# Sums of w_down's blocks made beside the q, k, v projection; a ring of their own for the sums of left blocks; squares of residual rows written to a row

## The chip, the core and the metric

The kernel runs on one core of a Trainium2 chip. The core has a matrix engine (TensorE, in the profile PE for matmuls and PEld for its weight loads), a vector engine (VectorE, DVE), a scalar engine (ScalarE, ACT), GpSimd (POOL) and SyncE (SP), which in this kernel issues every DMA. Each engine works through its own queue in order; semaphores hold an instruction until what it needs is there. The metric is the time of one execution on the device in microseconds, the median of several runs.

## The reference

One decoder layer over 2048 tokens of width 1024, all in float32:

```python
h = rmsnorm(x, g_mix);  z = h @ w_in                  # 1024 x 3072: conv columns and q, k, v
y_c = zb * causal_dwconv3(zc * zx, conv_w, conv_b)
y_a = dilated_attention(rmsnorm(q), rmsnorm(k), v)    # 8 heads, three dilated windows
x = x + concat(rmsnorm(y_c), rmsnorm(y_a)) @ w_out
h = rmsnorm(x, g_ffn)
gate = causal_dwconv3(h @ w_gate, ffn_conv_w, ffn_conv_b)
x = x + (silu(gate) * (h @ w_up)) @ w_down            # d_ff = 2816
x = x + sigmoid(rmsnorm(x, g_ple) @ w_ple_gate) * (p @ w_ple_proj)
```

## The kernel before

**Products.** Each float32 matrix is split in two parts, a high one (`hi`, made by a copy on ScalarE) and a low one (`lo`, the difference, made by VectorE or GpSimd); `split` (lines 90 to 92) does this, and `mm3` (94 to 99) multiplies with three matmuls: high by high, high by low, low by high. Matmuls are 128 x 128 by 128 x 512. The large products of the last part (`gate_up`, `down`, the gate of `ple`) use a scheme with seven instead of eight block products, for which sums and differences of blocks are made beforehand: the left operand's (`left`, 703), the right operand's (`right`, 728, seven tiles that are called the quad), and for `down` those of `silu(gate) * up` and of `w_down`.

**Stages.** `qkv` (first 334 us) goes over four chunks of 512 tokens (c) with four heads of work of 128 tokens each (j): `head` normalises x, transposes it, splits it and adds the two parts on GpSimd (line 174) to store h for the conv columns; `project` multiplies with w_q, w_k, w_v. `mix` then interleaves the conv group and the attention (to about 998 us). `rest` has the stages of line 655: `project` (the output projection, line 879; here and in the rest the name is that of the function in `rest`), `gate_up` for each half of the tokens (11 pairs f of 256 columns of d_ff, each with seven products for gate and seven for up), `down` for each half (seven products m of 11 f each), and `ple`. `prepare` and `for_later` are generators: `step()` takes one piece of them between products, as background work.

**w_down's sums.** `down` needs four sums of w_down's blocks (written to DRAM tiles `td`). They are made in `for_later`, the background of `gate_up 0`: eight pieces first normalise and transpose the other half's x into `bd`, then eleven pieces each load two blocks of w_down (256 rows), make four differences on GpSimd and store two tiles. All of these tiles come from the ring `operand("g")` (pool `rg`, four buffers of 4 KB a partition).

**Rings.** A tag's tiles go round in a fixed number of buffers. `row("t")` (pool `rx`, ten rows of 2 KB) serves in `gate_up` the four results t of each f and the three sums s1, s2, s4 of `combined` (a fourth is made in place), all of which go to DRAM (`gd`, lines 1015 and 1018); in `down` it serves the loads of gd (line 1041), which `split` turns into `operand("g")`; in `project` and `ple` rows of x and others. `row("u")` (pool `rs`, four rows) serves short-lived sums. `add_squares` (788) squares a row of the residual on ScalarE and adds it up; its elementwise result is not used and goes to `junk`, in `project` the PSUM bank of the product.

**Order.** The order of each engine's queue is not written by hand: the framework lays it out when the kernel is built, by the order of the code and by when it expects inputs and buffers to be there (`TileContext(nc, schedule_with_timeline_sim=True)`).

## Time and profile before

| | us |
|---|---|
| runs of the kernel before | 2870.42, 2872.03, 2878.88; median 2872.03 |
| profiled execution | 2883.12 |
| its span (first to last instruction) | 2881.3 |
| TensorE busy in the span | 2660.3 |
| q, k, v projection (0 to 334) | 334, TensorE 305.95 |
| mix (334 to 998) | 664, TensorE 607.33 |
| project (998 to 1251) | 253, TensorE 206.51 |
| gate_up 0 (1251 to 1724) | 473, TensorE 447.91 |
| down 0 (1724 to 1961) | 237, TensorE 216.38 |
| gate_up 1 (1961 to 2398.5) | 437.5, TensorE 432.18 |
| down 1 (2398.5 to 2645) | 246.5, TensorE 222.25 |
| ple (2645 to the end) | 236, TensorE 221.78 |

The table's stages are cut where TensorE changes from one group of tiles to the next. A busy matrix engine is not one at its peak: its clock has two levels, 2.4 and 1.2 GHz, and the share that was granted stands in the views by stretch as PEclk (1.00 is the upper level throughout). A row of a timeline gives start, duration, engine, line, operation, the tile written and the tiles read, how many like it were merged, and in brackets how long the engine was idle before it and what ended that.

### The profile page before, as it was taken

To read this page: it belongs to the slowest core of one execution; us is meant where nothing else is said; L and a number is where in the kernel's file an instruction comes from. 1 tells how busy PE (TensorE), PEld (TensorE's weight loads), DVE (VectorE), ACT (ScalarE), POOL (GpSimd) and SP (SyncE) were. 2 spreads that over 40 slices of the span, in tenths; PEclk is the share of its full clock that TensorE was granted. 3 is DMA by queue.
4 is the path that set the end of the run, shared out by engine and by line. 5 is a ranking of instruction groups with operands and counts; after the bars stand their busy time and mean duration, and the time that the engine had idled before them with its cause. 6 is when DMAs were issued, how large, how long until landed. Compare 5 with 4: busy or idle time off the path is not lost. (4 is left out here: it accounts for less than half of the span.)

```text
span 2881.3 us, 38272 instructions
## 1 busy us (share of the span) xinstructions
PE 2660.3 (92%) x12320; PEld 2194.4 (76%) x12320; DVE 2017.7 (70%) x3597; ACT 1291.1 (45%) x2699; POOL 1516.8 (53%) x1050
## 2 busy tenths in 40 slices
PE   6999989999999869799989998999999997998998
PEld 5777778888888757587767876877888886886777
DVE  7777656767676555978788777567888887657543
ACT  3332267776767234444333334453343334444332
POOL 4111311524344632446898667575666668667553
PEclk9999989999999989899999998999999998999999
DMA  6443666665765778544664237662232336674342
GB/s 182 147 139 117 183 152 145 184 167 156 188 160 160 192 258 275 162 166 146 233 217 154 91 127 235 218 228 92 99 106 99 103 109 211 228 240 160 96 127 77
DMA packets 374474, 470.11 MB, mean 163 GB/s; under 512 B 51072, under 2 KB 214528, under 8 KB 374272
## 3 DMA queue, kind: packets, MB, share of 16 engines
q1 hardware_dynamic: 374272, 467.66, 52.7%
q8 instruction: 97, 1.59, 0.2%
q14 instruction: 105, 0.86, 0.1%
HBM read 339.53 MB, written 127.99 MB: 162 GB/s over the span
## 5 line engine op out<-in xcount | busy, mean ns | idle before, releaser
L95 PE MATMUL ps<-t,w 128*128 128x512 f32 x4368 | 1040.9, 398 | 37.1 <-DVE u L766 19.1
L95 PEld LDWEIGHTS ps<-t,w 128*128 128x128 f32 x4368 | 824.7, 190 | 241.3 <-DVE u L766 22.2
L95 PE MATMUL ps<-w,g 128*128 128x512 f32 x2424 | 581.5, 401 | 77.3 <-ACT g L91 27.9
L92 POOL TENSOR_TENSOR w<-raw,w 128x512 fp32r<-128x512 f32 x318 | 469.7, 1483 | 322.5 <-ACT w L91 286.5
L95 PEld LDWEIGHTS ps<-w,g 128*128 128x128 f32 x2424 | 465.2, 194 | 187.5 <-ACT g L91 29.0
L92 POOL TENSOR_TENSOR w<-s,w 128x512 fp32r<-128x512 f32 x208 | 304.6, 1468 | 191.6 <-ACT w L91 182.8
L290 POOL TENSOR_TENSOR clo<-craw,chi 128x512 fp32r<-128x512 f32 x96 | 125.8, 1318 | 394.4 <-ACT chi L289 146.1
L91 ACT CAST w<-raw 128x512 fp32r<-128x512 f32 x318 | 196.0, 617 | 242.9 <-PE ps L95 157.6
L92 DVE TENSOR_TENSOR g<-t,g 128x512 fp32r<-128x512 f32 x154 | 207.8, 1360 | 126.4 <-ACT g L91 123.0
L95 PE MATMUL zps<-hq,chi 128*128 128x512 f32 x768 | 256.9, 412 | 7.4 <-DVE yc L329 5.0
L91 ACT CAST w<-s 128x512 fp32r<-128x512 f32 x208 | 128.0, 618 | 248.3 <-PE ps L95 179.7
L440 ACT ACTIVATE pt<-so,md 128x256 f32<-128x256 f32 (+1 forms) x384 | 175.0, 457 | 84.3 <-DVE md L437 82.3
L437 DVE CUSTOM_DVE_ANT_0 so<-s,neg 128x256 f32<-128x256 f32 (+1 forms) x384 | 130.5, 362 | 71.7 <-PE s L434 60.2
L95 PEld LDWEIGHTS zps<-hq,chi 128*128 128x128 f32 x768 | 142.3, 196 | 32.8 <-DVE yc L329 6.2
L95 PE MATMUL zps<-hq,clo 128*128 128x512 f32 x384 | 154.4, 403 | 0.0
L433 PE MATMUL s<-kk,qs 128*128 128x256 f32 (+1 forms) x384 | 134.4, 356 | 21.3 <-DMA kk<-kd 20.2
L434 PE MATMUL s<-kk,qs 128*128 128x256 f32 (+1 forms) x384 | 138.7, 365 | 15.2 <-DMA kk<-kd 9.6
L174 POOL TENSOR_TENSOR raw<-hT 128x1024 f32<-128x1024 f32 x16 | 39.0, 2440 | 202.2 <-DVE rs_h L78 187.4
L473 DVE TENSOR_TENSOR nb<-po,nb 64x512 f32<-64x512 f32 x96 | 92.2, 960 | 64.2 <-ACT nb L472 63.1
L1018 POOL TENSOR_TENSOR t<-t 128x512 f32<-128x512 f32 x88 | 126.5, 1449 | 5.9 <-DVE t L1010 3.2
L433 PEld LDWEIGHTS s<-kk,qs 128*128 128x128 f32 x384 | 106.9, 279 | 28.9 <-issue 14.5
L455 DVE TENSOR_TENSOR plo<-ptp,phi 128x512 fp32r<-128x512 f32 (+1 forms) x160 | 103.7, 654 | 32.0 <-ACT phi L454 31.1
(200 smaller groups left out, 4773.7 us busy)
## 6 DMA issues: line engine op xcount, KB each, us to landing
gd<-t SPq DMA_DIRECT2D x154, 256.0 KB, 2.0
t<-gd SPq DMA_DIRECT2D x154, 256.0 KB, 3.3
craw<-in_w_in_dram SPq DMA_DIRECT2D x96, 256.0 KB, 3.8
raw<-in_w_gate_dram SPq DMA_DIRECT2D x44, 512.0 KB, 3.9
raw<-in_w_up_dram SPq DMA_DIRECT2D x44, 512.0 KB, 3.6
raw<-td SPq DMA_DIRECT2D x40, 512.0 KB, 3.9
v<-vd SPq DMA_DIRECT2D x264, 64.0 KB, 2.5
kk<-kd SPq DMA_DIRECT2D x64, 256.0 KB, 8.0
```

The lines of the kernel that those rows point to most:

```text
L91: self.nc.scalar.copy(hi, src)
L92: lo_engine.tensor_tensor(lo, src, hi.bitcast(F32), ALU.subtract)
L95: mm = lambda *a, **k: self.nc.tensor.matmul(*a, **k, **kw)
L174: nc.gpsimd.tensor_tensor(t, hT[:, :, 0].bitcast(F32), hT[:, :, 1].bitcast(F32), ALU.add)
L290: nc.gpsimd.tensor_tensor(lo, raw, hi.bitcast(F32), ALU.subtract)
L433: mm(s[:, lo:], qb[l], cols[0], start=True, stop=False)
L434: mm(s[:, lo:], qb[l], cols[1], start=False, stop=True)
L437: nc.vector.tensor_tensor_reduce(out=so[:, lo:], in0=s[:, lo:], in1=neg[:, br, lo:], scale=-slope, scalar=3.0e38, op0=ALU.add, op1=ALU.min ...
L440: nc.scalar.activation(pt[:, l, lo:], so[:, lo:], AF.Exp, bias=md[:, 0, col:col + 1], scale=-1.0, accum_out=md[:, 1, col:col + 1])
L455: nc.vector.tensor_tensor(lo[:, i:i + n], tp[:, :n], hi[:, i:i + n].bitcast(F32), ALU.subtract)
L473: nc.vector.tensor_tensor(dst, like(po[other], br), dst, ALU.add)
L1018: nc.gpsimd.tensor_tensor(t, x, y, op)
```

## The change

Four edits. The eleven pieces of w_down's sums leave `for_later` and become `sums_of_w_down` in `qkv`, with two buffers of their own (tags `wd0`, `wd1`, one buffer each, 8 KB a partition together); one is called behind each of the first eleven heads of chunks 1 to 3. The sums s1, s2, s4 of `gate_up` get a pool of their own, `rk`, with three rows. To make room, ring `rg` goes from four buffers to three and ring `rx` from ten rows to nine. And the squares in `project` write to `row("u")` instead of the PSUM bank; the accumulator `sums` is renamed `squares`.

```diff
+            def sums_of_w_down(f):
+                b = [work.tile([P, 2, 512], F32, name="wd", tag=f"wd{i}", bufs=1) for i in range(2)]
+                for i, t in enumerate(b):
+                    n = (2 * f + i) * P
+                    nc.sync.dma_start(t.rearrange("p s n -> p (s n)"), a["w_down"][n:n + P])
+                minus = lambda t, x, y: nc.gpsimd.tensor_tensor(t, x, y, ALU.subtract)
+                (b11, b12), (b21, b22) = [[t[:, s] for s in range(2)] for t in b]
+                minus(b11, b12, b11)
+                minus(b12, b22, b12)
+                minus(b22, b22, b11)
+                minus(b21, b21, b22)
+                for d, t in zip(self.td, b):
+                    nc.sync.dma_start(d[f], t)
+
+            pairs = iter(range(NF // 2))
...
                     normed(project(hTs[j], 0), qn[j])
                     if c == 0 and j == 1:
                         load_w(1)
+                    for f in itertools.islice(pairs, int(c > 0)):
+                        sums_of_w_down(f)
...
-            late = pool("rg", bufs=4)
-            rows = pool("rx", bufs=10)
+            late = pool("rg", bufs=3)
+            rows = pool("rx", bufs=9)
+            sums = pool("rk", bufs=3)
...
-                                        add_squares(0, c, j, half, x, pss[j])
+                                        add_squares(0, c, j, half, x, row("u"))
...
-                minus = lambda t, x, y: nc.gpsimd.tensor_tensor(t, x, y, ALU.subtract)
-                for f in range(NF // 2):
-                    b1, b2 = wide(), wide()
-                    for i, b in enumerate((b1, b2)):
-                        n = (2 * f + i) * P
-                        nc.sync.dma_start(b.rearrange("p s n -> p (s n)"), a["w_down"][n:n + P])
-                    minus(b1[:, 0], b1[:, 1], b1[:, 0])
-                    minus(b1[:, 1], b2[:, 1], b1[:, 1])
-                    minus(b2[:, 1], b2[:, 1], b1[:, 0])
-                    minus(b2[:, 0], b2[:, 0], b2[:, 1])
-                    for t, b in zip(self.td, (b1, b2)):
-                        nc.sync.dma_start(t[f], b)
-                    yield
...
-                    s1, s2, s4 = (row("t") for _ in range(3))
+                    s1, s2, s4 = (sums.tile([P, 512], F32, name="c", tag="c") for _ in range(3))
```

## Rows read from the trace of the kernel before

**Rows 1.** The page: busy time of the engines (share of the span).

```profile
PE 2660.3 (92%) x12320; PEld 2194.4 (76%) x12320; DVE 2017.7 (70%) x3597; ACT 1291.1 (45%) x2699; POOL 1516.8 (53%) x1050
```

**Rows 2.** Busy time by stretch (instructions): gate_up 0's f = 2 to 6, one of gate_up 1.

```profile
core 0: us, PE busy (x) PEld busy (x) DVE busy (x) ACT busy (x) POOL busy (x), PEclk, DMA share, GB/s
1335.00:1377.50 42.50, 40.99 (x185) 33.05 (x184) 33.15 (x44) 16.91 (x29) 28.01 (x19) 1.00 0.45 155
1377.50:1428.60 51.10, 45.10 (x185) 35.94 (x184) 38.25 (x43) 17.13 (x29) 43.14 (x30) 0.90 0.66 235
1428.60:1478.40 49.80, 41.85 (x170) 33.34 (x169) 42.09 (x43) 14.72 (x24) 47.48 (x34) 0.90 0.65 213
1478.40:1523.90 45.50, 41.12 (x170) 32.51 (x169) 38.29 (x43) 15.27 (x25) 43.35 (x29) 0.96 0.68 229
1523.90:1566.60 42.70, 40.15 (x169) 31.00 (x168) 37.98 (x43) 15.24 (x26) 36.02 (x25) 1.00 0.44 155
2162.50:2201.80 39.30, 39.17 (x170) 31.52 (x169) 33.10 (x43) 15.08 (x25) 26.40 (x18) 1.00 0.30 100
1355.00:1550.00 195.00, 176.23 (x731) 140.10 (x730) 159.61 (x176) 66.51 (x112) 174.55 (x119) 0.94 0.61 211
```

**Rows 3.** Groups of POOL's instructions, 1355 to 1550 us: busy us, mean ns.

```profile
L965 POOL TENSOR_TENSOR g<-g 128x512 f32<-128x512 f32 x44 | 65.9, 1502 | 9.1 <-DMA g<-in_w_down_dram 8.8
```

**Rows 4.** Timeline of TensorE at the steps from gate_up to down.

```profile
1718.45 5.69 PE L95 MATMUL ps<-t,w 128*128 128x512 f32 x24 [0.87 <-DVE u L766]
1739.69 10.62 PE L95 MATMUL ps<-w,g 128*128 128x512 f32 x37 [15.55 <-ACT g L91]
...
2411.01 24.98 PE L95 MATMUL ps<-w,g 128*128 128x512 f32 x98 [12.36 <-ACT g L91]
```

**Rows 5.** Timeline of SP's DMA issues at the first of these steps.

```profile
1731.27 1.99 SPq L1015 DMA_DIRECT2D gd<-t  x2
1733.31 0.92 SPq L1041 DMA_DIRECT2D t<-gd  x2
```

**Rows 6.** Timeline of VectorE: the last result of up is taken from PSUM.

```profile
1726.28 0.68 DVE L1009 TENSOR_TENSOR u<-ps,u 128x512 f32<-128x512 f32 x1
...
2400.67 0.68 DVE L1009 TENSOR_TENSOR u<-ps,u 128x512 f32<-128x512 f32 x1
```

**Rows 7.** Busy time by stretch: the first step, and two of the projection (columns as above).

```profile
1727.00:1783.00 56.00, 40.60 (x161) 32.62 (x162) 42.94 (x34) 27.09 (x51) 42.76 (x28) 0.82 0.69 230
20.00:80.00 60.00, 48.05 (x196) 38.05 (x197) 55.34 (x139) 20.59 (x30) 29.04 (x12) 0.89 0.49 149
100.00:330.00 230.00, 226.02 (x1061) 182.43 (x1060) 170.06 (x510) 69.65 (x124) 41.89 (x22) 1.00 0.45 134
```

**Rows 8.** Timeline of POOL and VectorE in the projection.

```profile
117.76 2.44 POOL L174 TENSOR_TENSOR raw<-hT 128x1024 f32<-128x1024 f32 x1 [5.97 <-DVE rs_h L78]
...
117.95 2.34 DVE L80 TENSOR_SCALAR rs_y<-rs_i 128x8 int32<-128x8 int32 x2
```

**Rows 9.** Line 80 from 90 to 330 us: ns min/median/max.

```profile
L80 DVE TENSOR_SCALAR rs_y<-rs_i x34: 140/172/2300, 109.5 to 314.7; 128x8 int32<-128x8 int32 x24, 128x1 int32<-128x1 int32 x10
```

**Rows 10.** Timeline of SP's DMA issues at the start.

```profile
7.87 0.56 SPq L147 DMA_DIRECT2D gk<-in_k_norm_g_dram  x1
...
27.65 0.90 SPq L161 DMA_DIRECT2D raw<-in_w_in_dram  x2
```

**Rows 11.** Line 970, the 22 loads of w_down for the sums: time to landing.

```profile
DMA to landing us min/median/max: 3.3/4.8/5.4
```

**Rows 12.** What SP waited for, 1355 to 1560 us: in total, times, longest.

```profile
SPq L976 <- POOL g L965: 27.9, 16, 4.3
```

**Rows 13.** Timeline of ScalarE, VectorE and TensorE in the steady part of down 0.

```profile
1804.55 0.62 ACT L91 CAST g<-t 128x512 fp32r<-128x512 f32 x1
...
1805.26 1.31 DVE L92 TENSOR_TENSOR g<-t,g 128x512 fp32r<-128x512 f32 x1
...
1802.63 7.64 PE L95 MATMUL ps<-w,g 128*128 128x512 f32 x33
```

**Rows 14.** What TensorE waited for, whole span: in total, times, longest.

```profile
PE ps L95 <- DVE g L92: 9.8, 6, 2.7
```

More of the change, by code (lines that the diff above doesn't have):

```diff
@@ L784, in products @@
                 done(0, 1, z, u2)
-            sums = [cp.tile([P, 2, 4 * NQ], F32, name=f"sums{i}") for i in range(2)]
+            squares = [cp.tile([P, 2, 4 * NQ], F32, name=f"squares{i}") for i in range(2)]
             def add_squares(i, c, j, half, x, junk):
                 n = 4 * c + j
-                nc.scalar.activation(junk, x, AF.Square, accum_out=sums[i][:, half, n:n + 1])
+                nc.scalar.activation(junk, x, AF.Square, accum_out=squares[i][:, half, n:n + 1])
             def roots(i, first, n):
                 ss = tiny.tile([P, 8], F32, name="ssx", tag="ssx")[:, :n]
-                part = sums[i][:, :, first:first + n]
+                part = squares[i][:, :, first:first + n]
                 nc.vector.tensor_tensor(ss, part[:, 0], part[:, 1], ALU.add)
@@ L954, in for_later @@
                 r = roots(0, 8, 8)
-                wide = lambda: operand("g").bitcast(F32)
                 for j in range(4):
                     for i in range(2):
-                        x = wide().rearrange("p s n -> p (s n)")
+                        x = operand("g").bitcast(F32).rearrange("p s n -> p (s n)")
                         nc.sync.dma_start(x, self.xd[1][2 + i][j])
```

## The prediction

> **What bounds the kernel now.** I read the page first: TensorE is busy 92% of the span and no other engine over 70% [rows 1]. The change neither adds nor removes a matmul, so it can only move the time in which TensorE stands still or runs at its lower clock. Next I cut the span at the stages and looked for those with idle TensorE, and found two places that the change touches.
>
> The first lies in gate_up 0. An undisturbed f of gate_up 1 takes 39.3 us; in gate_up 0 four neighbouring f take 51.1, 49.8, 45.5 and 42.7 us [rows 2]. In the first three POOL is busy 84 to 95%, against 67% in the undisturbed f. POOL's groups of instructions there show what fills it: 44 subtractions for w_down's sums, 65.9 us [rows 3] of 174.6 busy in 195 us [rows 2]. POOL also makes the low part of each operand that TensorE waits for.
>
> The second is the step from gate_up to down, twice. TensorE stands 15.55 and 12.36 us, both times for ACT's split of g, and starts again slowly, with a lower granted clock [rows 7] (37 matmuls in 10.62 us against 24 in 5.69) [rows 4]. SP shows why: the first loads of g (t<-gd) are issued only behind the stores of the sums of the last f (gd<-t), and these wait for POOL [rows 5]. The "t" ring has ten rows; the last f holds seven, so three were free much earlier. That the loads came so late I take as a sign that rows of a tag are handed out in the order of the code: g comes after s1, s2, s4 of the last f.
>
> **The change, part by part.** The sum is made against the profiled execution, 2883.1 us (its span of 2881.3 and 1.8 around it), 0.4% over the median 2872.0 of the runs; the difference found is carried over to the median as a share.
>
> *A. The sums leave gate_up 0.* With 44 subtractions, 22 loads and 22 stores gone, nothing of for_later is left in f = 4 to 6, and f = 3 keeps only its 16 transposes, as the f before it, which took 42.5 us [rows 2]. Gain: (51.1 - 42.5) + (49.8 - 39.3) + (45.5 - 39.3) + (42.7 - 39.3) = 8.6 + 10.5 + 6.2 + 3.4 = 28.7 us. I take 29, ends 25 and 30. Nothing is late next: the same f of gate_up 1 runs at 39.17 busy of 39.30.
>
> *B. s1, s2, s4 get a ring of three; "t" has nine.* Four of the nine are the last f's, five are free, and in the order of the code g now follows the last f's gates. SP can issue five loads of g, and ACT and VectorE can split the three that the ring "g" takes, while TensorE is still at the last products. TensorE then waits only for its PSUM banks: the last result is taken out by 1727.0 and 2401.4 [rows 6], against starts at 1739.7 and 2411.0 [rows 4]. That is 12.7 + 9.6 = 22.3 us. With no long stall the clock stays up: 37 matmuls at 0.287 instead of 0.232 us and 98 at 0.255, 2.0 + 2.3 = 4.3 us. Together 26.6 at most. Against it: the background work (blocks for the next quad) still falls on these 56 us, in which VectorE was 42.9 and POOL 42.8 us busy [rows 7], and TensorE would now draw from them all through. I take 18, two thirds; ends 8 and 27.
>
> *C. The sums in the q, k, v projection (qkv).* Eleven pairs, one behind each head of c = 1 to 3 in the code. Each issues two loads and two stores of 512 KB on SP and four subtractions on POOL. POOL is not short: 41.9 of 230 us [rows 7]. VectorE is: 170 of 230 us there, and 55.3 of 60 us from 20 to 80 us [rows 7]. And POOL holds VectorE up: while the 2.44 us addition of L174 ran, two small instructions of L80 took 2.34 us, where the median of one is 0.17 and the longest 2.30 [rows 8, 9]. So an instruction of POOL costs VectorE between nothing and its whole length: 44 x 1.50 us [rows 3] = 66 us at most. I take half, 33.
> The Trainium skill, "SBUF — State Buffer", section "Who interferes with whom", has a rule against this change: GpSimd and some VectorE instructions (two SBUF inputs, or a two-port mode) lock a port pair for a whole instruction, and the other engine blocks fully. L80's rows agree in that the hold ends with POOL's instruction [rows 8]. By that rule alone the 66 us would stand whole, which is the third rival below.
> Where does it fall? Not where the code puts it. The loads of gk stand behind those of w1 and w2 in the code, and were issued at 7.9 us, ahead of w1's at 27.7 [rows 10]: work that waits for nothing is drawn forward. The sums wait for nothing but their two buffers. A pair takes a load (4.8 us to land [rows 11]), four subtractions (6.0 [rows 3]) and a store of the same size, some 15 us, so eleven reach from about 10 to 175 us. Four of them fall before 80 us: 16 x 0.75 = 12 us of VectorE's time against 4.7 idle, 7 on the path. Seven fall after: 28 x 0.75 = 21 us against an idle share of 26% of 95 us = 25, whose order does not fit exactly; a third, 7 us, on the path. The start also shares its DMA with 1 MB per pair, and on SP stand, behind each td store that waits for POOL, the next x loads, hd stores and spills; in gate_up 0 SP waited 27.9 us for those stores, 16 times [rows 12]. Another 3 us. Cost 17 us; ends 0 (all in idle time) and 58 (66 less a quarter of the 30 us idle).
>
> *D. Ring "g" of three, not four.* In down an operand takes 2.0 us from ACT's start to VectorE's end, and TensorE uses one for 12 x 0.232 = 2.8 us [rows 13]; its lead falls from about 6 (three more operands made, less 2.0) to 3.5 us. In steady stretches that is enough. With four, TensorE waited for VectorE's g six times, 9.8 us [rows 14]; each such place may grow by 2.8, 17 us at most, 0 at least. I take 8, the ple stage included, where a pair needs all three.
>
> *Answers at nothing.* Nine rows in project and in ple (a group takes four, so that two still fit), squares written to a "u" row instead of the PSUM bank (the bank comes free by one ACT instruction sooner; if "u" is short the square waits, not TensorE). The 8 KB more in the projection move the addresses of what follows; no row prices that, I leave 5 us either way in the range.
>
> Sum: -29 - 18 + 17 + 8 = -22 us, 2861 for a profiled execution, 0.76% less; of 2872.0 that leaves **2850**.
>
> **The rivals.** *All of it is won.* The sums fit into VectorE's gaps, the transitions close wholly: -29 - 27 + 3 = -53, 2819. For: from 100 us on TensorE had 226 of 230 us with VectorE a quarter idle [rows 7]. Against: 20 to 80 us.
> *The loads of g stay late.* If rows are not handed out in code order, or SP still has the stores in front, B does not do what it is meant to: -29 + 17 + 8 = -4, 2868, no change. For: SP issues in order, and 2 loads stood behind the first two stores. Against: the free rows.
> *The projection becomes bound by VectorE (slower).* Place: from 10 to 175 us. Each subtraction holds VectorE for its full length, and its instructions for the next head stand in a chain, so that only a quarter of the idle 30 us can be used: 66 - 8 = 58. With A, B and D as above -39 + 58 = +19, 2891. It decides from 48 us of cost on, 1.1 us per subtraction. For: L80's row, and 55.3 of 60 us. Against: the idle quarter from 100 us on.
>
> **How the numbers follow.** Forecast 0.50, all won 0.17, loads stay late 0.20, projection bound 0.13. A run of this kernel tells some 0.3% (8.6 us) from no change. Faster by more: 0.42 of the forecast, 0.17, and 0.06 of the late loads, 0.65. Within: 0.05 of the forecast and 0.13 of the late loads, 0.18. Slower: the rest, 0.17. Range 2815 to 2885: it takes in the first two rivals and the ends of A to D, and stops just short of the third.
>
> **What would show it.** A: gate_up 0's f = 4 to 6 at 39.3 us and POOL near 67%. B: loads t<-gd on SP ahead of the last gd<-t, a TensorE gap of 3 us or less at both steps, no low clock behind them. C: subtractions on POOL from about 10 us on, small VectorE instructions of 1 to 1.5 us, and the first 334 us longer by some 17; a projection of unchanged length means the first rival, one 50 us longer the third. D: more and longer waits of TensorE for VectorE's g in down. The prediction is wrong if the projection grows by more than A and B give, or if ple or the stage before gate_up moves by more than 5 us.

## The result and the profile after

| | before | after |
|---|---|---|
| median, runs of the comparison | 2874.62 us (4 runs, 2870.42 to 2878.88) | 2847.03 us (4 runs, 2841.30 to 2849.11) |
| ratio (95% interval) | | 0.9901 (0.9878 to 0.9924) |
| profiled execution, its span | 2883.1, 2881.3 us | 2848.68, 2846.9 us |
| granted clock, mean | 0.962 | 0.973 |

The change is worth 0.99%; forecast was 0.76%, 2850 us. The two profiled executions lie further apart than the medians (34.4 us against 27.6): that of before is 8.5 us above its median, that of after 1.7. One execution of experiment 6 (2990.68 us) and one of experiment 13 (2955.31 us) had a granted clock of 0.83 and 0.84 and do not count in the ratios.

The stages of both traces and of every experiment below, cut where TensorE changes from one group of tiles to the next (us; the experiments bear the numbers of their labels, and a "run" named in an expectation is the experiment of that number; there is none with number 4):

```
                     qkv    mix  project  gate_up0  down0  gate_up1  down1   ple    span
before             333.8  664.5    252.6     472.8  236.9     437.6  246.6  236.4  2881.3
after              363.3  655.3    239.9     446.4  232.2     440.0  235.0  234.9  2846.9
after - before      29.5   -9.3    -12.7     -26.4   -4.7       2.4  -11.7   -1.6   -34.4

e1_sums_moved      368.2  655.3    252.6     440.6  235.0     435.3  243.7  235.2  2866.0
e2_rings           333.2  658.1    254.2     483.6  231.9     440.8  234.0  231.5  2867.4
e3_squares         333.2  665.7    235.5     474.2  237.5     436.6  245.7  232.2  2860.5
e5_pool_only       360.8  660.4    255.5     473.9  236.0     435.4  245.4  233.5  2900.9
e6_dma_only        338.6  653.7    252.9     473.7  238.3     437.8  244.6  232.1  2871.7
e7_pinned          349.6  655.2    240.7     447.2  231.3     439.8  235.0  233.3  2832.0
e8_one_an_f        332.9  659.7    240.5     488.4  228.3     440.0  234.7  230.0  2854.6
e9_junk_row        334.1  660.5    258.9     472.0  237.7     436.5  246.9  233.9  2880.6
e10_beside_v       341.8  679.0    245.3     447.9  230.8     438.6  234.4  233.4  2851.1
e11_throttle       332.6  653.5    242.4     472.4  235.5     437.0  243.9  237.9  2855.1
e12_beside_v_early 353.2  652.3    243.5     446.4  229.6     440.9  236.3  230.4  2832.5
e13_own_queue      348.5  652.2    240.8     449.0  230.3     439.1  235.0  229.9  2824.8
```

In the kernels with the three rings of the change (after, 2, 7, 8, 10, 12, 13), 16 matmuls of the output projection run behind the first ones of gate_up 0. Some 3.7 us that the table counts to gate_up 0 are the output projection's there, so in after the two moved by some -9 and -30 rather than by -12.7 and -26.4.

The terms of the forecast's sum are there, one of them at nearly twice its size, and two stages moved that the forecast left at nothing.

**gate_up 0.** Busy time by stretch, after: f = 3 to 5, which answer to the slow f of [rows 2], and the stretch of 195 us.

```profile
core 0: us, PE busy (x) PEld busy (x) DVE busy (x) ACT busy (x) POOL busy (x), PEclk, DMA share, GB/s
1388.30:1428.90 40.60, 40.60 (x186) 33.13 (x185) 33.91 (x44) 17.07 (x29) 24.98 (x18) 1.00 0.36 124
1428.90:1469.10 40.20, 39.35 (x170) 31.42 (x169) 32.88 (x41) 14.77 (x25) 25.61 (x18) 1.00 0.31 98
1469.10:1508.30 39.20, 39.03 (x170) 31.44 (x169) 31.54 (x43) 14.76 (x25) 26.02 (x18) 1.00 0.32 102
...
1355.00:1550.00 195.00, 192.60 (x845) 155.16 (x844) 160.54 (x207) 75.87 (x130) 126.50 (x88) 1.00 0.35 117
```

The f that took 51.1, 49.8 and 45.5 us take 40.6, 40.2 and 39.2. POOL is busy 126.5 of 195 us where it was 174.55, and the granted clock is 1.00, where it was 0.94.

**The steps.** Timelines of TensorE after at both steps (they answer to [rows 4]), and of SP's issues at the first ([rows 5]).

```profile
1699.57 5.68 PE L95 MATMUL ps<-t,w 128*128 128x512 f32 x24 [0.88 <-DVE u L785]
1710.30 17.95 PE L95 MATMUL ps<-w,g 128*128 128x512 f32 x65 [5.05 <-ACT t L91]
...
2371.70 5.74 PE L95 MATMUL ps<-t,w 128*128 128x512 f32 x24 [1.62 <-DVE u L785]
2377.28 9.23 PE L95 MATMUL ps<-w,g 128*128 128x512 f32 x40
2388.71 11.56 PE L95 MATMUL ps<-w,g 128*128 128x512 f32 x43 [2.21 <-DVE g L92]
```

```profile
1691.22 2.36 SPq L1046 DMA_DIRECT2D t<-gd  x5
...
1697.45 1.62 SPq L1046 DMA_DIRECT2D t<-gd  x3
...
1713.28 0.32 SPq L1020 DMA_DIRECT2D gd<-c  x1
```

Eight loads of g go out 14 us and more ahead of the last four stores of gd, of which the first is at 1713.28 us; before, the first loads followed such stores. The gaps of 15.55 and 12.36 us are 5.05 and none, and the granted clock of the 56 us from the first step on is 0.91, where it was 0.82. The 5.05 stand for a split of the next quad (`t`), the background that the forecast had set against B. In down TensorE waits more often for VectorE's g, 19.0 us over the span (waits of TensorE; [rows 14] had 9.8):

```profile
PE ps L95 <- DVE g L92: 19.0, 9, 4.2
```

**The projection.** The sums as a tile's view tells them (duration min/median/max in ns, first and last start), with what POOL waited for; then two stretches of 50 us after, and the same two before.

```profile
L218 POOL TENSOR_TENSOR wd<-wd x44: 1260/1288/1319, 23.0 to 226.8; 128x512 f32<-128x512 f32 x44
L217 SPq DMA_DIRECT2D wd<-in_w_down_dram x22: 328/340/1198, 16.3 to 218.0; - x22
...
  DMA wd<-in_w_down_dram: 59.1, 16
```

```profile
80.00:130.00 50.00, 40.03 (x182) 31.52 (x181) 31.80 (x79) 15.37 (x28) 20.25 (x14) 0.96 0.70 231
...
180.00:230.00 50.00, 39.81 (x175) 31.57 (x176) 29.30 (x69) 14.40 (x27) 20.21 (x14) 0.91 0.84 278
```

```profile
80.00:130.00 50.00, 48.67 (x240) 39.29 (x240) 36.47 (x103) 18.97 (x34) 7.33 (x3) 1.00 0.57 173
...
180.00:230.00 50.00, 48.70 (x234) 39.18 (x233) 42.94 (x141) 15.59 (x29) 9.78 (x4) 1.00 0.47 137
```

As forecast, the pairs are drawn forward of their place in the code (first load at 16.3 us, chunk 0). TensorE loses until about 230 us and nothing afterwards, most in these two stretches, where it is busy 40.0 and 39.8 of 50 us for 48.7 before. Beside a subtraction the small instructions of the reciprocal roots last as long as it does, as L80 did in [rows 8]; timeline of POOL, then of VectorE, after:

```profile
141.92 4.04 POOL L218 TENSOR_TENSOR wd<-wd 128x512 f32<-128x512 f32 x3
...
142.03 1.26 DVE L80 TENSOR_SCALAR rs_y<-rs_i 128x8 int32<-128x8 int32 x2
...
143.35 1.26 DVE L83 SCALAR_TENSOR_TENSOR rs_u<-rs_y,rs_h 128x1 f32<-128x1 f32 x1
...
144.65 1.33 DVE L87 SCALAR_TENSOR_TENSOR rs_y<-rs_u,rs_y 128x1 f32<-128x1 f32 x2
```

One held instruction takes 1.3 us instead of 0.2; between two subtractions one or two slip through. All 528 instructions of the roots in this stage took 144.9 us before and 165.2 after (their durations added up). SP's queue moved too: the four loads of x that follow chunk 0's projection of v are issued at 131.87 us, 15 us later than before. TensorE itself was 8.9 us late by then (the last product of v of chunk 0 starts at 113.6 us for 104.7), so the rest of the 15 is the queue's. SP's timeline, after and then before:

```profile
131.87 2.59 SPq L69 DMA_DIRECT2D xt<-in_x_dram  x4
```

```profile
116.72 3.56 SPq L69 DMA_DIRECT2D xt<-in_x_dram  x4
```

### The profile page after: what moved, and what is told of

It is laid out like the page before. It is cut to its first block, busy times and chain, and to the rows that moved or that the text cites. A ratio compares the mean times of both kernels' runs of the same rounds, so it can differ in the third digit from the quotient of the medians.

```text
span 2846.9 us, 38253 instructions
## 1 busy us (share of the span) xinstructions
PE 2649.6 (93%) x12320; PEld 2180.7 (77%) x12320; DVE 2005.4 (70%) x3597; ACT 1284.3 (45%) x2699; POOL 1508.8 (53%) x1050
## 5 line engine op out<-in xcount | busy, mean ns | idle before, releaser
L95 PE MATMUL ps<-t,w 128*128 128x512 f32 x4368 | 1027.7, 395 | 19.6 <-DVE u L785 10.3
L92 DVE TENSOR_TENSOR g<-t,g 128x512 fp32r<-128x512 f32 x154 | 201.2, 1314 | 118.8 <-ACT g L91 116.9
L451 PE MATMUL s<-kk,qs 128*128 128x256 f32 (+1 forms) x384 | 132.7, 352 | 16.3 <-DMA kk<-kd 15.3
L734 DVE TENSOR_TENSOR s<-raw 128x512 f32<-128x512 f32 x88 | 94.2, 1071 | 46.7 <-POOL w L92 45.5
L995 ACT ACTIVATE t<-t 128x512 f32<-128x512 f32 x88 | 55.3, 629 | 158.7 <-DVE t L276 155.3
L274 ACT ACTIVATE t<-e,fcb,fcw 128x512 f32<-128x512 f32 x88 | 69.5, 810 | 123.5 <-DVE e L267 123.5
```

What stands on the lines that cost most here:

```text
L92: lo_engine.tensor_tensor(lo, src, hi.bitcast(F32), ALU.subtract)
L95: mm = lambda *a, **k: self.nc.tensor.matmul(*a, **k, **kw)
L274: nc.scalar.activation(t, ext[:, 0:QT], AF.Identity, scale=w[:, 0:1], bias=b)
L451: mm(s[:, lo:], qb[l], cols[0], start=True, stop=False)
L734: nc.vector.tensor_tensor(t, x, y, op)
```

## The experiments

**The parts alone.** Three kernels do one edit each on the kernel before.

*Experiment 1: the sums moved, nothing else.*

```diff
+            def sums_of_w_down(f): ...           # as in the change, called behind the heads of chunks 1 to 3
-                for f in range(NF // 2):          # the eleven pieces of for_later
-                    ...
```

> The kernel before with the sums moved alone; rings and squares as before. Theory (the edits act each in its own stage): the projection some 30 us longer, gate_up 0 some 27 us shorter, both steps from gate_up to down still with gaps of 15 and 12 us; in all -5 to +5 us. Rival (the 9 us that mix and the 13 us that project won in the changed kernel come from the moved sums as well): about -20 us.

Measured: 2859.31 us, ratio 0.9943 (0.9926 to 0.9961). gate_up 0 gains 32.2 us, the projection of q, k, v loses 34.4: in the two stages that it touches the moving by itself buys nothing. What the whole gained all the same, 16.3 us by the medians, lies in mix (-9.2) and in small parts of the later stages; the expected -5 to +5 us of the whole are missed by that.

*Experiment 2: the rings alone, sums still in gate_up 0.*

```diff
-            late = pool("rg", bufs=4)
-            rows = pool("rx", bufs=10)
+            late = pool("rg", bufs=3)
+            rows = pool("rx", bufs=9)
+            ring = pool("rk", bufs=3)
-                    s1, s2, s4 = (row("t") for _ in range(3))
+                    s1, s2, s4 = (ring.tile([P, 512], F32, name="c", tag="c") for _ in range(3))
```

> The kernel before with the rings alone: three rows for s1, s2, s4, ring g three, ring t nine; the sums stay in gate_up 0. Theory: the gaps at the two steps fall from 15.6 and 12.4 us to 5 and 2, waits for VectorE's g in down grow by some 9 us, in all -12 to -18 us; gate_up 0 as before within 3 us. Rival (the steps closed because the sums had left gate_up 0): gaps as before, 0 us or worse.

Measured: 2869.46 us, ratio 0.9982 (0.9969 to 0.9994). The steps close without the sums having gone: TensorE's gap at the first is 4.17 us for a split of the next quad, and down 0, gate_up 1 and down 1 together give -14.4 us (after: -14.0). TensorE's waits for VectorE's g are 19.1 us, as in after. gate_up 0 loses 10.8, some 7 of them its own, where no more than 3 were expected. That with the sums still in it a ring of three for x and the pairs is too small is a reading of this; no run took it apart. The whole gained 6.2 us by the medians, not the 12 to 18 expected.

*Experiment 3: the squares alone.*

```diff
-                                        add_squares(0, c, j, half, x, pss[j])
+                                        add_squares(0, c, j, half, x, row("u"))
```

> The kernel before with the squares written to a row alone. Theory: the 13 us that project won in the changed kernel come from here, since a PSUM bank comes free sooner: project about 240 us instead of 253, all else as before, -12 us. Rival (project was won by another edit or by the order in which SP's issues fell): 0 to -3 us.

Measured: 2859.65 us, ratio 0.9938 (0.9919 to 0.9957). The output projection takes 235.5 us for 252.6: the one line that the forecast answered at nothing pays by itself as much as the moving (16.0 us against 16.3 by the medians). The three parts alone come to 38 us, the change to 28, so they do not add up; mix, for one, counts -9.2 us in experiment 1 and -6.4 in experiment 2. What the line removes shows in part in the waits of TensorE from 1000 to 1256 us, before:

```profile
PE tp L812 <- DVE rsy L853: 8.3, 1, 8.3
```

20 transposes of the background stand in a row on TensorE's queue and wait for VectorE, which is full just there. In experiment 3 they are spread out, four to eight at a time, and 1.2 us is left of such waits. Two readings: the product's bank comes free sooner (after VectorE's addition, no longer after the square), or the squares' draw on the four "u" rows holds back the preparation, which uses the same ring.

**Which of the two (experiments 9 and 11).** The first frees the bank and draws no "u" row, the second draws a "u" row and frees no bank.

```diff
+            junk = cp.tile([P, 512], F32, name="junk")            # experiment 9; rows 10 -> 9 to pay for it
-                                        add_squares(0, c, j, half, x, pss[j])
+                                        add_squares(0, c, j, half, x, junk)
```

```diff
                                         add_squares(0, c, j, half, x, pss[j])
+                                        nc.scalar.copy(row("u")[:, :1], x[:, :1])   # experiment 11
```

> The kernel before, with the squares of the residual rows written to one row of their own in SBUF (2 KB, paid for with nine residual rows for ten, which cost the stage +1.6 us with the rings alone) in place of the product's bank in PSUM, and no row drawn from the ring of the u rows. It tells two readings of the third experiment apart, where the stage of the output projection fell from 252.6 to 235.5 us. Theory 1 (the product's bank comes free after VectorE's addition, no longer after the square on ScalarE, so that the next products are ordered and issued earlier): the stage falls as much, to 234 to 240 us, the whole to 2856 to 2864 us. Rival (the squares take places in the ring of u rows and hold back the preparation that crowded VectorE ahead of the scale): the stage stays at 248 to 256 us, the whole at 2868 to 2876 us.

> The kernel before with the squares written to the product's bank as before, and behind each square one copy of a single column on ScalarE into a row drawn from the ring of the u rows (32 copies more, nothing of before left out). It tells what the third experiment gained the output projection's stage. Theory 1 (the squares' draw on the u ring holds back the preparation that crowded VectorE; the bank's time of release has no part): the stage falls from 252.6 to 234 to 242 us though the bank comes free as late as before, the whole to 2856 to 2866 us. Rival (both are needed, the draw on the ring and the bank free after VectorE's addition, or the order came out well by chance of the two): the stage stays at 248 us or more, the whole at 2868 us or more.

Measured: experiment 9 at 2876.64 us, ratio 1.0005 (0.9987 to 1.0022), stage 258.9 us; experiment 11 at 2854.60 us, ratio 0.9929 (0.9903 to 0.9955), stage 242.4 us. The stretch from 1150 to 1200 us in before, in 9, in 3 and in 11 (columns as above), and after these the wait in 9:

```profile
1150.00:1200.00 50.00, 35.96 (x169) 28.64 (x169) 48.12 (x77) 27.91 (x55) 25.97 (x19) 0.86 0.42 135
```

```profile
1150.00:1200.00 50.00, 37.95 (x170) 29.20 (x169) 47.80 (x75) 28.03 (x53) 26.33 (x19) 0.86 0.40 129
```

```profile
1150.00:1200.00 50.00, 43.28 (x204) 34.01 (x203) 46.29 (x87) 23.96 (x50) 16.43 (x12) 0.97 0.66 205
```

```profile
1150.00:1200.00 50.00, 44.76 (x200) 35.56 (x200) 43.29 (x75) 25.20 (x58) 14.88 (x12) 0.92 0.62 195
```

```profile
PE tp L813 <- DVE rs_u L85: 6.5, 1, 6.5
```

The bank alone wins nothing: the stall stays, TensorE is busy 38 of 50 us. (Experiment 9 also has nine rows for ten; nine rows together with the other rings cost the stage 1.6 us in experiment 2, by its own matmuls some 5, so the nine rows may be the 6.3 that it lost.) The draw on the ring alone, which costs 32 copies more, gives 10.2 of the 17.1 us and spreads POOL's and VectorE's work as experiment 3 does. The pacing can be seen: the background's eight copies into "u" rows (u<-tp) end 196 and 198 us behind the stage's start in before and in 9, 217 in 3 and 227 in 11. A shortage of buffers that spreads the background out, and not the bank, is the cause for that part. Whether the other 7 us are the bank's once the background is paced, or the copies' cost, was not tried.

**What the projection of q, k, v lost.** Theory: GpSimd holds VectorE. Rival: the pairs' transfers and SyncE's queue.

*Experiment 5: the 44 subtractions alone,* on tiles of zeros, with no load and no store, beside the kernel before. The sums proper stay in gate_up 0.

```diff
+            wd = [...]                                    # two tiles, set to zero once
+            def sums_of_w_down(f):                        # called as in the change
+                pinned(minus(b11, b12, b11), self.added)  # ordered on GpSimd behind L174 of its head
+                minus(b12, b22, b12)
+                minus(b22, b22, b11)
+                minus(b21, b21, b22)
```

> The kernel before with 44 subtractions more on GpSimd in the projection, on two tiles of zeros, four behind each of the first eleven heads of chunks 1 to 3, without any DMA; the sums proper stay in gate_up 0. Theory (VectorE held by POOL makes the projection longer): VectorE's instructions some 24 us longer in all and the projection longer by 10 to 24 us. Rival (the loads and stores on SP and the DMA engines make it longer): under 5 us.

Measured: 2903.18 us, ratio 1.009 (1.007 to 1.011); the stage takes 360.8 us, 27.0 more. Here four and more subtractions run in a row. Timeline of POOL, then of VectorE:

```profile
144.58 8.06 POOL L224 TENSOR_TENSOR wd<-wd 128x512 f32<-128x512 f32 x6
...
144.68 1.27 DVE L80 TENSOR_SCALAR rs_y<-rs_i 128x8 int32<-128x8 int32 x2
145.93 0.17 DVE L85 TENSOR_TENSOR rs_u<-rs_y 128x8 f32<-128x8 f32 x1
146.01 1.26 DVE L83 SCALAR_TENSOR_TENSOR rs_u<-rs_y,rs_h 128x1 f32<-128x1 f32 x1
147.19 0.15 DVE L86 TENSOR_TENSOR rs_u<-rs_u,rs_h 128x8 f32<-128x8 f32 x1
147.31 1.30 DVE L87 SCALAR_TENSOR_TENSOR rs_y<-rs_u,rs_y 128x1 f32<-128x1 f32 x2
```

Two steps of a chain for each subtraction. The roots come to 187.3 us (144.9 before), and TensorE's wait for VectorE's hT grows from 7.5 us to:

```profile
PE ps L95 <- DVE hT L125: 24.5, 9, 4.3
```

*Experiment 6: the 22 loads and 22 stores alone.*

```diff
+                    nc.sync.dma_start(t.rearrange("p s n -> p (s n)"), a["w_down"][n:n + P])
+                for d, t in zip(self.sd, b):      # scratch tensors; no subtraction between
+                    nc.sync.dma_start(d[f], t)
```

> The kernel before, with the 22 loads and 22 stores of the moved sums put beside the projection of q, k and v as in the change, the stores going to scratch tensors that nobody reads, and with no subtraction there; the sums proper stay in gate_up 0. Theory 1 (what the projection lost with the change is GpSimd's hold on VectorE, and the transfers and SyncE's queue are a few us of it): the projection goes from 333.8 to 336 to 339 us and the whole to 2875 to 2881 us. Rival (the longer waits for vd and kd, some 30 us of ScalarE's and SyncE's idle time in the trace after, stand on the path): the projection is at least 345 us, the whole 2885 us or more.

Measured: 2873.51 us, ratio 0.9995 (0.998 to 1.001); the stage takes 338.6 us, 4.8 more. The transfers by themselves are cheap. But no store waited for a subtraction here, as it does in the change.

*Experiment 7: the change, with no pair drawn forward into chunk 0.*

```diff
-                minus(b11, b12, b11)
+                pinned(minus(b11, b12, b11), self.added)   # `pinned` and `self.added` as in experiment 5
```

> The changed kernel with the first subtraction of each pair ordered on GpSimd behind the addition L174 of the head beside which it is written, so that no pair is drawn forward into the first chunk; loads and stores are as in the change. Theory 1 (each of the 44 subtractions holds VectorE wherever it stands): the projection stays at 358 to 366 us, the whole within 5 us of the changed kernel. Rival (the cost is that pairs drawn forward to 23 us and later stand in the way of the weights' and operands' first preparation): the projection falls to 345 us or less, the whole to 2825 to 2832 us.

Measured: 2832.26 us, ratio 0.9847 (0.9817 to 0.9876), 15 us better than the change. The stage takes 349.6 us, between the two expectations: the drawing forward was worth 13.7 us, half of the loss. It is not VectorE that was relieved: the roots came to 181.0 us, more than the 165.2 of the change. SP's queue was, at the change of the chunks: the first subtraction is at 111.4 us, and the loads of x are back near their old time. In sum SP waits for the pairs no less (61.0 us, in the change 54.0), but none of these waits falls between 107 and 114 us, ahead of the loads of x at the first change of chunks, and only 3.9 us fall between 172 and 231, around the second. Timeline of SP, and the stretch from 80 to 130 us:

```profile
118.34 0.35 SPq L69 DMA_DIRECT2D xt<-in_x_dram  x1
```

```profile
80.00:130.00 50.00, 45.88 (x219) 36.90 (x218) 36.48 (x89) 17.61 (x31) 11.48 (x7) 0.97 0.66 202
```

*Experiment 10: the pairs beside the projections of v of chunks 1 to 3,* where VectorE's own work takes its operands from PSUM.

```diff
                     ps = project(hTs[j], 2)
+                    for f in itertools.islice(pairs, int(c > 0)):
+                        sums_of_w_down(f)         # first subtraction waits for the projection's first product
```

> The changed kernel with the eleven pairs written beside the projections of v (chunks 1 to 3, one to a projection) in place of those of q, and the first subtraction of each pair waiting for the first product of that projection. Theory 1 (what a subtraction costs depends on what VectorE has in hand: its work beside v takes its operands from PSUM, vt<-ps at 422 to 424 ns a piece in the traces of before, after and of the pinned pairs alike, while the reciprocal roots beside q, all in SBUF, are lengthened two- to threefold): the projection stage takes 336 to 344 us, the whole 2815 to 2828 us, faster than the pairs pinned beside q (2832.26 us). Rival (the roots of the next chunk run beside v as well, so that the 44 subtractions hold VectorE as much there): the stage at 348 us or more, the whole at 2830 us or more.

Measured: 2856.55 us, ratio 0.9936 (0.9917 to 0.9955). The stage is as the theory had it, 341.8 us, 8.0 over before and with roots of 158.3 us, but only 36 of the 44 subtractions lie in it; the next one lost 14.4. TensorE's start of the attention, and SP's and POOL's timelines there:

```profile
391.34 0.44 PE L457 MATMUL s<-kk,qs 128*128 128x128 f32 x1 [18.69 <-DMA kk<-kd]
...
379.67 3.02 SPq L231 DMA_DIRECT2D td<-wd  x2
...
384.05 1.25 SPq L425 DMA_DIRECT2D kk<-kd  x2
...
378.38 3.94 POOL L224 TENSOR_TENSOR wd<-wd 128x512 f32<-128x512 f32 x3 [1.92 <-DMA wd<-in_w_down_dram]
```

The last pair's store stands on SP ahead of the loads of k and waits for the last subtraction. One late store holds a whole stage: TensorE waits 18.69 us here, 7.5 before.

*Experiment 12: the same beside v in chunks 0 to 2.*

```diff
-                    for f in itertools.islice(pairs, int(c > 0)):
+                    for f in itertools.islice(pairs, int(c < NQ - 1)):
```

> The kernel of the tenth run with the pairs written beside the projections of v in chunks 0 to 2 (four, four, three) in place of 1 to 3, so that the last subtraction and its stores are done before the stage of the convolution and the attention begins. Theory 1 (beside v a pair costs 8.0/11 = 0.7 us, and the 14.4 us that the next stage lost in the tenth run is its late start, where TensorE waited 18.69 us for kk loaded from kd whose stores stood on SyncE's queue behind the last pairs): the projection stage at 338 to 346 us, the next stage back at 653 to 660 us, the whole 2816 to 2828 us, faster than both kernels and than the pairs pinned beside q (2832.26 us). Rival (beside v of chunk 0 the pairs meet VectorE where it is fullest, 56 of 60 us at 20 to 80 us, and cost as much as beside q): the projection stage at 348 us or more, the whole at 2830 us or more.

Measured: 2835.01 us, ratio 0.9860 (0.9834 to 0.9885). The next stage is back (652.3), but the projection takes 353.2 us, as the rival had it, though not for the rival's reason: the roots are at 157.4 us, the least of all kernels with the subtractions there, and chunk 0 is only 2.6 us longer. Waits of ScalarE from 20 to 350 us, then of SP:

```profile
ACT vt L91 <- DMA vd<-vt: 22.1, 4, 8.4
ACT qhl L207 <- DMA kd<-qhl: 21.1, 3, 8.9
ACT hn L111 <- DMA xt<-in_x_dram: 19.2, 5, 6.0
```

```profile
SPq L223 <- DMA td<-wd: 34.3, 11, 4.4
...
SPq L231 <- POOL wd L224: 20.7, 8, 6.1
```

SP stands 55 us in all for the pairs, about as long as in the change and in experiment 7; what counts is what is queued behind, which here comes late to ScalarE.

*Experiment 13: the same, the pairs' transfers issued by GpSimd.*

```diff
-                    nc.sync.dma_start(...)        # both, loads and stores of the pairs
+                    nc.gpsimd.dma_start(...)
```

> The kernel of the twelfth run (pairs beside the projections of v in chunks 0 to 2) with the 22 loads and 22 stores of the pairs issued by GpSimd in place of SyncE. Theory 1 (what the twelfth run still lost beside v, 19.4 us, is SyncE's queue: a store of a pair that waits for its subtraction, 20.7 us in 8 times, and a load that waits for the pair before to be stored, 34.3 us in 11, hold the loads of x and the stores of qd, kd and vd behind them, and ScalarE waits 19.2 us for xt, 22.1 for vd and 21.1 for kd): the projection stage falls to 335 to 343 us, the whole to 2812 to 2824 us. Rival (it is GpSimd's subtractions themselves, by holding VectorE or by what queues behind them on GpSimd, where the waits for the pairs' transfers now stand too): the stage stays at 348 us or more, the whole at 2830 us or more.

Measured: 2826.59 us (three executions), ratio 0.9838 (0.9797 to 0.9879). The stage takes 348.5 us, only 4.7 less than in 12, and the theory is missed on that. SP is free of the pairs, but now the roots are longer (170.4 us, 13.0 more than in 12): the subtractions fell on other places of VectorE's chain. By this reading one cause was exchanged for a part of the other; no run shows it apart.

*Experiment 8: the sums in gate_up 0 after all, one pair to an f.* Nothing of them in the projection.

```diff
                     combined(6, s4, a12, s2, ALU.subtract)
+                    for n in () if h else range(f, f + 1) if f < 8 else (8, 9) if f == 8 else (10,) if f == 9 else ():
+                        sums_of_w_down(n)         # in ring "g", ordered behind this f's last combination
```

> The changed kernel with the sums back in gate_up 0, but one pair to an f (two at f 8, one at f 9), each ordered on GpSimd behind the last combination of its f, in the ring of g; nothing of them beside the projection of q, k and v. Theory 1 (in gate_up 0 the sums cost what they delay the combinations and the evictions by when two pairs fall on one f; GpSimd has 8 to 10 us left in an f of 39.3 us, where a pair takes 5 to 6): the projection is back at 333 us, gate_up 0 takes 446 to 460 us, the whole 2822 to 2836 us, faster than both kernels. Rival (a pair costs VectorE its 2.5 us in gate_up too, where VectorE is as busy, and its loads hold up the ring of three for g): gate_up 0 at 470 to 482 us, the whole 2842 to 2854 us, no faster than the changed kernel.

Measured: 2856.76 us, ratio 0.9939 (0.9915 to 0.9963). gate_up 0 takes 488.4 us, worse than the 472.8 of before and than both expectations; f = 5 to 8 take 43.4 to 43.9 us each instead of 39.3. TensorE's waits in that stage, in 8 and then in after:

```profile
PE ps L95 <- DVE u L767: 28.5, 10, 4.6
```

```profile
PE ps L95 <- DVE u L785: 3.2, 9, 0.9
```

POOL has 13 us free in each f of after, yet a pair put into each costs 3.8 us of TensorE's time ((488.4 - 446.4) / 11). 25 of the 42 us are waits for VectorE, which takes the results out of PSUM later; the rest, to which the pairs' draw on ring "g" may belong, was not taken apart. Beside q, k, v a pair costs 2.7 us as the change has it, 1.4 pinned (experiment 7).

## Why the prediction was right, and where it was not

**A, the sums leave gate_up 0: right.** 29 us forecast, 26.4 measured in the change (some 30 without the output projection's last products) and 32.2 alone, with f = 4 to 6 at 39.2 to 40.2 us and POOL busy 26 us in each.

**B and D: right, a little too small.** The forecast was -18 and +8, together -10. Down 0, gate_up 1 and down 1 gave -14.0, and ple another -1.6. D is as forecast: 9.2 us more of waiting for VectorE's g (19.0 against 9.8). That leaves some 23 to B by the sum, near its upper end of 27. The loads went out early, as the forecast had taken from the order of the code, so the rival of late loads is out; experiment 2 shows it without the other parts. Two of B's signs failed at the first step: the gap was to be 3 us or less and is 5.05, and the granted clock behind it is 0.91.

**C, the projection: the direction right, the size not.** Forecast +17 (14 for VectorE, 3 for transfers and SP), measured +29.5. The step that failed is "another 3 us". Where the pairs would fall was off as well, without changing the sum much: the subtractions took 1.29 us each, not 1.50, ran from 23 to 228 us, not from about 10 to 175, and 8 of them lie before 80 us, not 16. (And a pair moves 2 MB, loads and stores together, where the forecast names 1.) The rise of the roots in each trace, set against what the stage lost (us):

```
                     roots    more than before   stage longer by
before               144.9
e5_pool_only         187.3          42.4               27.0
e7_pinned            181.0          36.1               15.8
e10_beside_v         158.3          13.4                8.0
e13_own_queue        170.4          25.5               14.7
after                165.2          20.3               29.5
e1_sums_moved        161.1          16.2               34.4
e12_beside_v_early   157.4          12.5               19.4
e6_dma_only          140.2          -4.7                4.8
```

In the first four, 44 to 64% of the lengthening shows in the stage, 64% in experiment 5, which has no transfers. The next three lose more than all of their lengthening. By that share the lengthening in after, 20.3 us and 3 more in L113 (23.5 us against 20.5), is worth some 10 to 15 us, which is the 14 of the forecast (reached from 33 us lengthened, at 42%). The remaining 15 to 19 us go to the queue, where the forecast had 3. The three traces that VectorE explains least are those whose loads of x behind chunk 0 are latest: 134.5 us in experiment 1, 131.87 in after and 127.23 in experiment 12, against 116.72 before and 118.34 in experiment 7.

Chunk by chunk it shows more plainly (us longer than before, from the start of one chunk's last product of v to the next; then how much longer the roots are, and the subtractions that fall there):

```
               chunk 0           chunk 1           chunk 2           chunk 3
after          8.9   6.8  16     9.0  11.4  20    11.7   2.2   8    -0.1   0.0   0
e7_pinned     -0.4   0.3   0     4.4  12.8  16     5.3  11.9  16     6.5  11.1  12
e5_pool_only  -1.2   0.1   0    10.3  15.8  16    10.1  15.2  16     7.8  11.4  12
```

Chunk 2 of after loses most with the fewest subtractions and 2.2 us of longer roots. At its start a store of v (vd) goes out on SP behind a store and a load of the pairs; ScalarE waits 4.82 us for that store, the pieces of k (qhl) behind it in ScalarE's queue come late, and TensorE stands 3.83 us where it stood 0.26 before. Timelines of SP, ScalarE and TensorE after, then of TensorE before:

```profile
193.62 0.70 SPq L225 DMA_DIRECT2D td<-wd  x1
194.42 1.20 SPq L217 DMA_DIRECT2D wd<-in_w_down_dram  x1
195.67 1.12 SPq L257 DMA_DIRECT2D vd<-vt  x1
...
203.09 0.37 ACT L91 CAST vt<-ps 128x256 fp32r<-128x256 f32 x1 [4.82 <-DMA vd<-vt]
...
204.90 1.11 PE L199 MATMUL qt<-ident,kn 128*128 128x128 f32 x4 [3.83 <-DVE qhl L207]
```

```profile
183.44 0.66 PE L199 MATMUL qt<-ident,kn 128*128 128x128 f32 x4 [0.26 <-DVE qhl L207]
```

The forecast had named the mechanism (x loads, hd stores and spills behind a store that waits for POOL) and priced it from the sum of SP's waits in gate_up 0, where nothing stood behind them that TensorE needed soon. So the queue is shown as a cause. The split, 10 to 15 and 15 to 19, is worked out from shares; it was not measured by a run that takes the one cause away and leaves the other as it is. Experiment 13 was to be that, and VectorE's share rose in it.

The Trainium skill, "SBUF — State Buffer", section "Who interferes with whom", says that VectorE's instructions with two SBUF inputs and GpSimd's that read SBUF block each other wholly, and that VectorE does not contend with at most one SBUF input outside its two-port modes. The traces agree on the kind: the roots, all in SBUF, last 1.26 to 1.33 us beside a subtraction of 1.29, while hT<-tp,hT (one input from PSUM) stays at 679 to 692 ns in the ten cases of after in which GpSimd runs beside it. L79 and L80 have one input and are held as well; by the page that would be their two-port mode, which no run here shows. The full price that the forecast drew from the rule did not come: of 44 x 1.29 = 56.7 us, 12 to 42 appear as lengthening of the roots. The third rival, which took the full price, is out.

**Answers at nothing: wrong for the squares.** The forecast looked at what the edit frees (a bank, sooner) and at who waits for the bank, and wrote that if "u" is short the square waits, not TensorE. "u" did become short, and what was held back was the background that shares the ring, which was a gain of 12.7 us in the change (some 9 by the stage's own matmuls) and 17.1 alone. The sentence that the prediction is wrong if the stage before gate_up moves by more than 5 us has come true for this term.

**Mix, -9.3 us: seen, its reason open.** Its instructions are untouched. Of the 9.3 us, 2.4 are less idle time of TensorE and 6.8 are less busy time for the same matmuls (607.8 and 601.0 us), with a mean granted clock of 0.946 before and 0.964 after; 665.7 us in experiment 3 go with 0.946 too, 653.5 in experiment 11 with 0.969. So most of it is the granted clock. What set it is open: leaving out experiment 10, whose mix starts late for a known reason, the stage takes 652.2 to 665.7 us over thirteen traces, at most 655.3 in the six with the pairs' transfers in qkv and 658.1 or more in six of the seven others, but 653.5 in experiment 11, which has neither the sums nor new rings. The forecast's 5 us for moved addresses was too narrow a bound for that, and how much a second profile of one kernel would differ was not measured.

So that the time came out, 2847.03 for 2850, is luck in part. Between the profiled executions, on which the sum was made, the change is worth 34.4 us where the forecast had 22: C was 12.5 us dearer and A 2.6 us smaller than forecast, B and D 5.6, the squares 12.7 and mix 9.3 us better. The medians lie 27.6 us apart, nearer to the forecast, since the profiled execution of before lay 8.5 us above its median.

**A faster version.** Experiments 7, 12 and 13 are all faster than both kernels, 0.9847, 0.9860 and 0.9838 of before; the longest execution that counts of the three took 2836.6 us, the shortest of the change 2841.3. The intervals overlap, and which of them is the fastest these runs don't tell. Experiment 7 is one ordering more than the change.

## What to carry to other kernels

Work that is moved to an idle engine is to be priced by the queues that it joins: a store that waits for a slow engine holds up every load behind it on an in-order queue, and one that stands ahead of the next stage's loads costs that stage its start. Work whose inputs are free at the start is drawn forward to where the kernel is tightest, so give it an order of its own (one ordering was worth 15 us here). And look at who else draws on a ring before calling a change of buffers free: a ring that is short can pace background work to advantage, as a longer one can let it crowd in. Before a stage whose instructions are untouched is given a cause, compare its granted clock: here it made up most of 9 us.

## What the runs showed of the hardware

A chain of small VectorE instructions goes at the pace of GpSimd's large ones beside it: while six subtractions ran in a row in 8.06 us, VectorE finished about two instructions per subtraction, one at 1.26 to 1.33 us and one at its usual 0.15 to 0.23 (experiment 5). The hold does not go by size: 128x1 elements are held as long as 128x8.

Between a large VectorE instruction with two inputs in SBUF, hn<-xt,rs_y,g_mix (128x1024, 1.28 us alone), and a GpSimd instruction, the one that started first went at its own pace and the other was held until it ended. In experiment 7 a subtraction started at 134.72 us and took 1.31, and hn, started 0.19 us later, took 2.21; in experiment 13 hn started at 198.02 us and took 1.29, and the subtraction, started 0.19 us later, took 2.21.
